# Nested self-attention on one core: a piece for 512- and 480-row pairs that runs on in class 448, and order lists with written-out PSUM banks

## The chip, the cores and the metric

The kernel runs on one core of one Trainium2 chip. The metric is the device time of one launch in microseconds; lower is better. The time of the kernel before is the median of three runs on the chip.

## What is computed

Thirty-two sequences of 64 to 511 valid rows, each 512 wide, go through a self-attention of 8 heads of 64 with one fused projection matrix. Rows behind a sequence's length are zero in the output.

```python
for b in range(batch):
    seq_len = lengths[b]
    x_b = x[b, :seq_len].copy()
    qkv = np.matmul(x_b, w_qkv)
    q, k, v = np.split(qkv, 3, axis=-1)
    ...
    scores = scale * np.matmul(q, k.transpose(0, 2, 1))
    scores_max = np.max(scores, axis=-1, keepdims=True)
    attn = np.exp(scores - scores_max)
    attn = attn / (np.sum(attn, axis=-1, keepdims=True) + 1e-08)
    out_b = np.matmul(attn, v).transpose(1, 0, 2).reshape(seq_len, dim)
    output[b, :seq_len] = out_b
```

The kernel takes the exponential without subtracting a maximum. The sums come out of the product with `v`, which carries a column of ones.

## The kernel before, in words

**Pairs and classes.** The device sorts the lengths in falling order and handles the sequences two at a time: pair p holds ranks 2p and 2p+1, and the first of the two is called batch 0 (or the first half), the second batch 1 (the second half). A pair's class is the longest length rounded up to one of 15 sizes (`CLASSES`: 512, 480, 448, ..., 96, and 340 between 352 and 320). For each class there is unrolled code for one pair. The lengths of this draw, sorted, are 502 447 | 446 436 | 363 357 | 351 347 | 343 333 | 323 315 | 310 261 | 260 257 | 246 230 | 223 220 | 216 183 | 164 152 | 143 140 | 134 119 | 101 86 | 79 75, so the pairs run in classes 512, 448, 384, 352, 352, 340, 320, 288, 256, 224, 224, 192, 160, 160, 128 and 96.

**A half.** `make_body(N, M, W)` writes the program of a pair for TensorE, ScalarE and VectorE. N is the row count at which batch 0 is worked, M that of batch 1, W that of the batch after it. In each half, the attention of the current batch is interleaved with the projections (Q, K and V) of the next one. There are three bodies for a class: `stay` (N, N, N), `leave` (N, N, next lower class) and, for some classes, `drops` (N, lower, lower), which works batch 1 already in the lower class. In the kernel before a drop exists where the lower class has as many 128-row tiles and N is at most 384; here pairs 4 (352 to 340), 5 (340 to 320), 6 (320 to 288), 10 (224 to 192) and 11 (192 to 160) take one. The function `graph` lays the pieces out and branches between them by a code per pair that is read from a table (2 × class, plus 1 for a drop). On TensorE, a jump can be announced ahead by a branch hint.

**Order of the work.** Inside a half the order is a hand-written string of tokens (`ORDER`, `DENSE`, `FOUR`), the same for all three engines; each engine runs its own instructions of it strictly in that order. `S` is the score matmuls of a unit and the exp on ScalarE that reads them; `D` the same for the dense three-tile classes, where both score slots are filled at once; `Q`, `K` project one of Q and K for one of the four pairs of heads, `B` both of them in one bank (two-tile classes); `E` and `F` to `I` are a projection of Q and K that is split in two by rows of the contraction (64 rows each, two matmuls side by side in the array); `V` projects one tile of V; `A` (and `Z`) are the products with V; `R` and `X`, the reciprocal and the multiplication on VectorE; `O` issues the store of half a batch from ScalarE's queue and reads the index of the batch it goes to (L1522 to L1527); reading the next pair's code is L1241 to L1245.

**PSUM and waits.** `psc` holds two score slots, s0 and s1; four more banks, a0, a1, v0 and v1, take projections and products with V. Whoever empties a bank raises its semaphore `e_<bank>`, and the next group of matmuls that writes the bank waits for it (`acquire`). In three- and four-tile classes up to 448 rows, the banks are handed out by turns: `pick` takes the first (with `~` the second) of a list, `give` puts the bank at its end, and the list runs on from the first half into the second. A group that starts a half thus gets the bank that was used longest ago. Classes 512 and 480, and the two-tile classes, use a0 and a1 for projections and v0 with v1 for products with V. In a two-tile half the scores of the next batch's first pair of heads are worked ahead: the units are pairs 1, 2, 3 and then 0 of the next batch.

**Moving data.** SyncE issues the loads of x, the transposing DMAs and the zero fills; GpSimd casts x and writes the ones. The change leaves both as they are, but for one constant in GpSimd's set-up.

The lines that the steps below touch: L324 is every matmul (`mm`), L367 and L408 the exps, L439 and L440 the copies of Q and K out of PSUM on ScalarE and VectorE, L463, L559 and L560 the masked copies of V, L638, L659 and L661 reciprocal and multiplication, L1527 the store.

## Time and profile before

| what | value |
|---|---|
| time, median of 3 runs | 333.07 us (332.78 to 334.8) |
| span of the profiled execution | 330.1 us; its own time is not among the three, and 333.07 less 330.1 leaves 3.0 us around the span |
| TensorE busy | 316.4 us, 96% of the span |
| ScalarE busy | 242.4 us, 73% |
| VectorE busy | 203.6 us, 62% |
| granted TensorE clock, mean | 0.991 |
| first pair (512) | 24.56 to 62.84 us |
| pair 1 (448) | 62.84 to about 98 us |
| seven dense halves (340 to 288) | 159.7 to 235.4 us |
| six two-tile pairs (256 to 160) | 235.4 to 310.7 us |

In a timeline row stand the start, the duration, the engine (a small q marks its sequencer), the line, the operation, out<-in, and the shapes; an x4 merges four instructions. The end of a matmul is modelled and overlaps the next, so the time that a group takes on TensorE is read from its start to the start of the next group. Rows of windows give busy time and count of each engine, then the granted clock, the DMA share and the traffic.

### The profile page before, as it was taken

To read this page: it belongs to the slowest core of one execution; us is meant where nothing else is said; L and a number is where in the kernel's file an instruction comes from. 1 tells how busy PE (TensorE), PEld (TensorE's weight loads), DVE (VectorE), ACT (ScalarE), POOL (GpSimd) and SP (SyncE) were. 2 spreads that over 40 slices of the span, in tenths; PEclk is the share of its full clock that TensorE was granted. 3 is DMA by queue.
4 is the path that set the end of the run, shared out by engine and by line. 5 is a ranking of instruction groups with operands and counts; after the bars stand their busy time and mean duration, and the time that the engine had idled before them with its cause. 6 is when DMAs were issued, how large, how long until landed. Compare 5 with 4: busy or idle time off the path is not lost. (4 is left out here: it accounts for less than half of the span.)

```text
span 330.1 us, 12320 instructions
## 1 busy us (share of the span) xinstructions
PE 316.4 (96%) x4353; PEld 205.5 (62%) x4354; DVE 203.6 (62%) x587; ACT 242.4 (73%) x358; POOL 68.7 (21%) x135
## 2 busy tenths in 40 slices
PE   7899999999999999999999999999999999999880
PEld 2565445455565656656666677677777777677750
DVE  3576576656585575576476557655755566767662
ACT  4577878788889879878778887787677676566531
POOL 3452220201111201210220222022111131131331
PEclk9999999999999999999999999999999999999996
DMA  6957599987656996985997999897689979965952
GB/s 195 341 138 263 94 375 310 292 179 279 153 194 142 326 263 145 323 286 149 283 314 169 235 319 216 214 291 235 212 139 174 214 199 183 170 201 148 200 145 70
DMA packets 83289, 72.42 MB, mean 219 GB/s; under 512 B 41660, under 2 KB 64188, under 8 KB 83204
## 3 DMA queue, kind: packets, MB, share of 16 engines
q1 hardware_dynamic: 69700, 58.27, 70.0%
q10 hardware_dynamic: 13504, 13.11, 11.8%
q8 instruction: 42, 0.69, 0.8%
q14 instruction: 43, 0.35, 0.4%
HBM read 25.32 MB, written 36.70 MB: 188 GB/s over the span
## 5 line engine op out<-in xcount | busy, mean ns | idle before, releaser
L367 ACT ACTIVATE ep<-psc 128x896 f16<-128x896 f32 (+9 forms) x184 | 146.8, 847 | 44.0 <-PE psc L324 34.0
L324 PE MATMUL pa<-xT,w_r 128*128 128x160 f16 (+19 forms) x952 | 127.8, 277 | 1.2 <-PEq L62 1.2
L324 PEld LDWEIGHTS pa<-xT,w_r 128*128 128x128 f16 (+1 forms) x952 | 73.0, 97 | 29.2 <-issue 10.1
L324 PE MATMUL psc<-qkT 64*128 64x224 f16 (+17 forms) x700 | 66.7, 285 | 0.6 <-ACT ep L408 0.4
L324 PE MATMUL pa<-w_r,xT 128*128 128x512 f16 (+4 forms) x332 | 58.6, 328 | 0.3 <-DVE v_aug L560 0.3
L324 PE MATMUL pav<-xT,w_r 64*128 64x352 f16 (+12 forms) x384 | 58.3, 306 | 0.0
L440 DVE CAST qkT<-pa 128x512 f16<-128x512 f32 (+9 forms) x59 | 33.4, 566 | 40.0 <-PE pa L324 36.2
L408 ACT ACTIVATE ep<-psc 128x864 f16<-128x864 f32 (+3 forms) x56 | 49.7, 946 | 10.9 <-PE psc L324 6.5
L324 PE MATMUL pav<-v_aug,ep 128*128 128x65 f16 x1268 | 54.9, 194 | 1.7 <-PEq L62 1.7
L1968 POOL MEMSET v_aug<- 128x256 f16 x28 | 8.8, 313 | 225.5 <-POOLq L1519 225.5
L324 PEld LDWEIGHTS pav<-v_aug,ep 128*128 128x128 f16 x1268 | 48.8, 98 | 10.0 <-issue 3.0
L439 ACT CAST qkT<-pa 128x320 f16<-128x320 f32 (+8 forms) x74 | 34.2, 466 | 16.6 <-PE pa L324 10.8
L661 DVE SCALAR_TENSOR_TENSOR onat<-pav,masks,rcp 128x128 f32<-128x128 f32 (+1 forms) x120 | 41.4, 384 | 4.1 <-DVE rcp L638 1.6
L1962 POOL CAST x<-x_nat 128x1536 f16<-128x1536 f32 (+3 forms) x33 | 42.0, 1272 | 8.6 <-POOLq L1519 8.3
L324 PEld LDWEIGHTS psc<-qkT 64*128 64x128 f16 x700 | 26.7, 94 | 27.2 <-issue 16.7
L463 DVE TENSOR_TENSOR v_aug<-pa,masks 128x512 f16<-128x512 f32 (+1 forms) x46 | 30.8, 674 | 15.0 <-PE pa L324 14.4
L324 PEld LDWEIGHTS pav<-xT,w_r 64*128 64x128 f16 (+1 forms) x384 | 29.8, 95 | 11.6 <-issue 1.6
L324 PEld LDWEIGHTS pa<-w_r,xT 128*128 128x128 f16 (+2 forms) x332 | 22.9, 99 | 18.3 <-issue 4.9
L324 PE MATMUL pav<-w_r,xT 128*128 128x512 f16 (+3 forms) x132 | 24.0, 333 | 0.0
L638 DVE RECIPROCAL rcp<-pav 128x8 f32<-128x8 f32 (+2 forms) x66 | 12.9, 195 | 17.5 <-PE pav L324 14.7
L324 PEld LDWEIGHTS pa<-v_aug,ep 128*128 128x128 f16 x524 | 19.3, 98 | 6.3 <-issue 2.6
L440 DVE CAST qkT<-pav 128x352 f16<-128x352 f32 (+7 forms) x27 | 14.4, 539 | 14.1 <-PE pav L324 13.4
(99 smaller groups left out, 181.4 us busy)
## 6 DMA issues: line engine op xcount, KB each, us to landing
out_dram<-zt SPq DMA_DIRECT2D x16, 768.0 KB, 5.7
x_nat<-in_x_dram SPq DMA_DIRECT2D x12, 512.0 KB
out_dram<-onat ACTq DMA_DIRECT2D x21, 256.0 KB, 3.8
x_nat<-in_x_dram SPq DMA_DIRECT2D x5, 1024.0 KB
out_dram<-onat ACTq DMA_DIRECT2D x12, 384.0 KB, 4.8
out_dram<-onat SPq DMA_DIRECT2D x12, 384.0 KB, 4.4
x_nat<-in_x_dram SPq DMA_DIRECT2D x17, 256.0 KB, 6.5
x_nat<-in_x_dram SPq DMA_DIRECT2D x4, 768.0 KB
```

Of the source, the lines that this page charges most:

```text
L324: return lambda e: e.matmul(o, lhsT, rhs, start=start, stop=stop)
L367: return e.activation(out=dst[at], in_=src[at], func=AF.Exp, scale=scale)
L408: lambda e, par=par, b=b: e.activation(out=ep[:, i, par, 0:T, 0:N], in_=psc_f[:, par, 0 : T * N].rearrange("p (t n) -> p t n", n=N), func= ...
L439: return lambda e: e.copy(out=dst, in_=src)
L440: return lambda e: e.tensor_copy(out=dst, in_=src)
L463: return lambda e: e.tensor_tensor(out=v_aug[h][:, t, lo // HD : lo // HD + n, 0:HD], in0=area[b][:, 0:w].rearrange("p (a d) -> p a d", d=HD),
L638: pr.add("dve", lambda e: e.reciprocal(out=rv, in_=den).then_inc(s_r, 1))
L661: ins = e.scalar_tensor_tensor(scalar=now[0][:, 1, t : t + 1], op0=ALU.mult, op1=ALU.mult, **ops)
L1962: e.tensor_copy(out=x16[h][:, 0:T, :], in_=x_nat[h][:, 0:T, :]).then_inc(s_xc[h], 1)
L1968: e.memset(v_aug[h][:, T - 1, NPAIR:NH, 0:HD], 0.0)
```

## The change

Every half is now written out with its banks. `LISTS` replaces `ORDER`, `DENSE` and `FOUR` for classes above 256 rows; `TWO` holds two lists for two-tile classes. A token names its banks behind a colon, and its engine by a letter (d VectorE, a ScalarE). The same list serves the first and the second half; `pick`, `give`, `turn` and the table of banks that was carried on are gone. The list of the dense classes, for example, has the banks that the turns gave to the first half before.

```diff
+    LISTS = {
+        512: "S e1:v0,a0 S E1da S e2:v1,a1 S c E2da S e0:v0,a0 S e3:v1,a1 S E0da E3da S S A00:v0 R00 X00 A01:a0 R01 X01 V1d:v1 A10:a1 R10 X10 S S A11:v0 R11 X11 V3d:a0 A20:v1 R20 X20 S O S V0d:a1 A21:v0 R21 X21 S A30:a0 R30 X30 A31:v1 R31 X31 S S V2d:a1",
...
+        288: "K2d:a0 Q2a:a1 D e1:v0,v1 e3:a0,a1 E1aa E3ad D K0a:v0 c A00:v1 R00 X00 Q0d:a1 A10:a0 R10 X10 D V2d:v0 O V1d:v1 A20:a1 R20 X20 D A30:v0 R30 X30 V0d:a0",
     }
-        4: "S S Q0 +A0 S S K0 V0 S S Q1 +A1 S S K1 V1 S S Q2 +A2 S S K2 V2 S S Q3 +A3 S S V3 K3 O",
-        2: "S S B0 b1 A0 A1 b2 S S V1 b3 A2 O A3 R3 X3 V0",
-    DENSE = "K2 q2 D E1 E3 I1 H3 D k0 c A0 Q0~ A1 D V2 O V1 A2 D A3~ V0"
-    DENSE_OUT = DENSE.replace("D A3~ V0", "V0 D A3")
+    TWO = {
+        False: "S1 S0 e0:a0,a1 e1:v0,v1 E0d E1d S2 S3 A00:a0 A01:a1 R0 X00 X01 V0d:v0 V1d:v1 A20:a0 A21:a1 R2 X20 X21 B2a:v0 c B3d:v1 O",
+        True: "S1 S0 e0:a0,a1 e1:v0,v1 E0d E1d S2 S3 V1d:a0 A00:v0 A01:v1 R0 X00 X01 B2a:s0 A20:a0 A21:a1 R2 X20 X21 V0a:v0 c B3d:v1 O",
+    }
```

In a two-tile half all four pairs of heads now have their scores in the half itself (S1 S0 first, S2 S3 later), two of the projections are split by rows (`two_cross`) and emptied two banks at a time by VectorE, and two pairs of heads share a bank for the product with V (`two_attn`). The second list is for batches whose last tile has at most 64 rows; there V0 is masked and copied by ScalarE (`v_out` and `vsides` have a form for it).

```diff
+    def two_cross(pr, h, i, bs, W, engs=None):
+
+        last = engs is not None
+        mms = [m for pair in zip(*(
+            qk_mms(bs[f], h, [(i, f)], W, MAXS, ROWS[f ^ last], not last, last)
+            for f in range(2)
+        )) for m in pair]
+        done, n = s_crossed[i], len(mms) - 2
+        if last:
+            pr.take("pe", done, 2)
+        else:
+            for b in bs:
+                acquire(pr, b)
...
+        eng = engs[0]
+        for b in bs:
+            pr.take(eng, full[(b, eng)])
+            pr.busy[b] = bs[0]
+        pr.joined.update({bs[0]: bs[1], bs[1]: bs[0]})
+        src, dst = two_banks(bs)[:, :, 0:W], qkT[h][:, 2 * i : 2 * i + 2, 0:W]
+        pr.add(eng, lambda e: (e.copy if eng == "act" else e.tensor_copy)(
+            out=dst, in_=src).then_inc(free[bs[0]], 1))
```

The part that gives the change its name: classes 512 and 480 get a drop to 448. The prologue marks the jump to the first of these pieces ahead.

```diff
-    drops = {N: make_body(N, lower[N], lower[N], turn=turn(N)) for N in CLASSES
-             if lower[N] < N and -(-lower[N] // P) == -(-N // P) and N <= 3 * P}
-    drops_to = [lower[N] for N in drops]
+    drops_at = {N: M for N, M in lower.items()
+                if M < N <= 3 * P and (-(-M // P) == -(-N // P))}
+    drops_at.update({N: FOUR_ROWS for N in CLASSES if N > FOUR_ROWS})
+    drops = {N: make_body(N, M, M) for N, M in drops_at.items()}
+    drops_to = list(drops_at.values())
...
+            if tok == "V2":
+                pr.add("pe", hint_drop)
...
+    def hint_drop(e):
+        e.reg_alu(regs["far"], regs[e.engine][1], 1, ALU.not_equal)
+        regs["opened"] = e.mark_branch_hint_location(regs["far"])
...
-        marks = {}
+        marks = {("tail", -1, 1): [regs["opened"]]} if fetch else {}
```

In this draw pair 0 (502 and 447 rows) takes the new piece. Its first half is worked at N = 512 and projects 448 rows of batch 1, its second half is class 448 throughout; before, the two halves were 512 with 512 rows projected, and 512 with 480.

Two places show how the order moved. The first is TensorE at the end of the first half of a 288-row pair (pair 7): the last V projection of the half and, behind the branch, the first projection of the second half. Names with _0 and _1 are the two batches' buffers; e_a0 and e_v1 are raised when those banks are empty. Before:

```order
L324 MATMUL pa<-w_r,xT_1 128x512 [waits e_a0]
L324 MATMUL pa<-w_r,xT_1 128x512 x3
L1311 REGISTER_ALU
L1312 BRANCH_PREFETCH_HINT
L1331 COMPARE_AND_BRANCH
L1311 REGISTER_ALU
L1312 BRANCH_PREFETCH_HINT
L1311 UNCONDITIONAL_BRANCH
L324 MATMUL pav<-xT_0,w_r 128x288 [waits s_xt0,e_v1]
L324 MATMUL pav<-xT_0,w_r 128x288 x3
L324 MATMUL pa<-xT_0,w_r 128x288 [waits e_a1]
```

The same place with the change:

```order
L333 MATMUL pa<-w_r,xT_1 128x512 [waits e_a0]
L333 MATMUL pa<-w_r,xT_1 128x512 x3
L1474 REGISTER_ALU
L1475 BRANCH_PREFETCH_HINT
L1494 COMPARE_AND_BRANCH
L1474 REGISTER_ALU
L1475 BRANCH_PREFETCH_HINT
L1474 UNCONDITIONAL_BRANCH
L333 MATMUL pa<-xT_0,w_r 128x288 [waits s_xt0,e_a0]
L333 MATMUL pa<-xT_0,w_r 128x288 x3
L333 MATMUL pa<-xT_0,w_r 128x288 [waits e_a1]
```

The V projection writes a0 in both; the K projection behind it took v1 and now takes a0 again. The matmuls are the same.

The second place is ScalarE in a first half of a pair in class 224, from the middle of the half to the first exps of the second half; idx and codes are the tables of batch indices and of class codes, s_of00 says that the first half of batch 0's output is complete. Before:

```order
L1241 ISA
L1245 TENSOR_LOAD codes
L367 ACTIVATE ep<-psc 128x2x2x224 [waits f_s0_act]
L367 ACTIVATE ep<-psc 128x2x2x224 [waits f_s1_act]
L439 CAST qkT_1<-pa 128x2x224 [waits f_a0_act]
L1522 ISA
L1523 TENSOR_LOAD idx
L1524 ISA
L1527 ISA [waits s_of00]
L1527 DMA out_0_dram<-onat_0 128x2x256
L1495 COMPARE_AND_BRANCH
L367 ACTIVATE ep<-psc 128x2x2x224 [waits f_s0_act]
```

With the change:

```order
L376 ACTIVATE ep<-psc 128x2x2x224 [waits f_s1_act]
L448 CAST qkT_1<-pa 128x2x224 [waits f_v0_act]
L1403 ISA
L1407 TENSOR_LOAD codes
L1694 ISA
L1695 TENSOR_LOAD idx
L1696 ISA
L1699 ISA [waits s_of00]
L1699 DMA out_0_dram<-onat_0 128x2x256
L1667 COMPARE_AND_BRANCH
L376 ACTIVATE ep<-psc 128x2x2x224 [waits f_s0_act]
L376 ACTIVATE ep<-psc 128x2x2x224 [waits f_s1_act]
```

The copy of a projection that stands ahead of the store is now that of B2, whose matmuls are the last but one group of the half; the code is read behind it and no longer two exps earlier. The exps behind the branch are those of S1 and S0, on which S2 and S3 of the same half wait on TensorE.

More of the change, by code (lines that the diff above doesn't have):

```diff
@@ L795, in half @@
-            return
-        per = T if T >= 3 else 1
-        ahead = tiles if T >= 3 else 1
-        units = [(i, k) for i in (1, 2, 3) for k in range(per)] + [(0, k) for k in range(ahead)]
-        norm, dones, both = {}, 0, []
-        dense, turns = is_dense(N), in_turns(N)
-        four = FOUR_SIDES if tiles == T and half_rows(W) else FOUR
-        toks = ((DENSE_OUT if tiles < T else DENSE) if dense else four if T == 4 and turns else ORDER[T]).split()
-        def pick(second=False):
-            if turns:
-                b = st["banks"].pop(1 if second else 0)
-                st["seen"].add(b)
-                st["holds"].pop(b, None)
-                return b
-            st["bank"] ^= 1
-            return f"a{st['bank'] ^ 1}"
@@ L938, in is_dense, with make_body @@
         return -(-N // P) == 3 and 3 * N <= 2 * MAXS
-    def in_turns(N):
-        return 2 * P < N <= FOUR_ROWS
-    def make_body(N, M, W, last=False, turn=None):
+    def make_body(N, M, W, last=False):
         T = -(-N // P)
         pr = Prog(CANON, 0)
-        first = ("v0", "a0", "v1", "a1") if T == 4 else tuple(area)
-        st = {"slot": 0, "bank": 0, "banks": list(first), "seen": set(), "holds": {}}
+        st = {"slot": 0, "seen": set(), "holds": {}, "two": False}
         for h in range(2):
@@ L1306, in graph @@
         drop = [N in drops for N in CLASSES]
+        to = [CLASSES.index(drops_at.get(N, lower[N])) for N in CLASSES]
         assert tiles[n - 3 :] == [2, 1, 1]
```

686 lines of the change are left out of this document (410 added, 276 removed), and 8 rows, old and new, of tables (LISTS, ORDER).

## The prediction

> **What bounds the kernel now.** I read the page's busy times first, then the windows by stage, then the timelines of TensorE, VectorE and ScalarE where the order changes.
>
> ```profile
> PE 316.4 (96%) x4353; PEld 205.5 (62%) x4354; DVE 203.6 (62%) x587; ACT 242.4 (73%) x358; POOL 68.7 (21%) x135
> ```
>
> ```profile
> 24.56:43.95 19.39, 19.39 (x210) 9.47 (x210) 12.42 (x28) 15.50 (x16) 4.31 (x4) 1.00 0.71 197
> 43.95:62.84 18.89, 18.89 (x209) 9.61 (x208) 12.48 (x34) 15.24 (x16) 2.29 (x3) 1.00 1.14 314
> 62.84:80.43 17.59, 17.57 (x245) 10.05 (x245) 10.89 (x33) 14.33 (x20) 2.29 (x3) 1.00 0.88 263
> ...
> 159.71:235.38 75.67, 75.06 (x1158) 53.30 (x1158) 47.44 (x157) 60.03 (x91) 12.51 (x19) 1.00 0.92 240
> 235.38:310.67 75.29, 74.96 (x1084) 56.62 (x1084) 47.93 (x128) 51.92 (x85) 17.86 (x36) 1.00 0.87 186
> ```
>
> The first number is the stretch, the second TensorE's busy time. In every stage the two are equal to within 0.6 us, at granted clock 1.00: TensorE never waits, and the other engines have a quarter or more of each stage to spare. Two things follow. What shortens TensorE's own work is gained in full. And every wait that the new order puts in front of a TensorE group is lost in full, since no slack is there to take it up. So I look at each piece for fewer columns, and for new waits.
>
> **The new 512 piece** (pair 0). It does less work. The first half of pair 1 (third row of the windows) is the same list at N = 448 with 448 rows projected: 17.59 us. The new second half is just that, 17.59 against 18.89: 1.30 gained. The new first half is that plus 64 more score columns in 24 matmuls. Pairs of them run side by side:
>
> ```profile
> 58.15 0.58 PE L324 MATMUL psc<-qkT 64*128 64x480 f16 x4
> 58.66 0.38 PE L324 MATMUL pa<-xT,w_r 128*128 128x480 f16 x1
> ```
>
> Four of 480 columns take 0.51 us, so 64 more columns in 24 take 24/4 x 0.51 x 64/480 = 0.41; 18.0 us against 19.39, 1.39 gained. Against that, the K copies (E1da, E2da, E0da, E3da) go to ScalarE, which before had exps alone there:
>
> ```profile
> 67.43 0.54 ACT L439 CAST qkT<-pa 128x448 f16<-128x448 f32 x1
> ```
>
> The 15.50 us of 16 exps in the first row of the windows (0.97 each) and four such copies are 17.7 us in 18.0: nearly full. The first seven exps and two copies are 7 x 0.97 + 1.08 = 7.9 us, while TensorE brings seven score units in about 7 us; two slots of buffer leave a wait of some tenths, which I put at 0.3 (0 if the queue keeps up, 1.0 if it starts late). The piece gives 1.30 + 1.39 - 0.3 = **-2.4 us**. Pair 1 has the same list and the same turn of banks as before: 0.
>
> **The dense halves** (340 to 288 rows, seven in all). The matmuls are the same. But one list now serves both halves, and it ends with V0 in bank a0 and begins with K2 in bank a0. K2 has to wait until VectorE has copied V0 out, behind the last product's reciprocal and multiplications. Before, the turns gave K2 another bank. The old trace tells when that copy ends, since VectorE's order is unchanged. Here are TensorE's K2 behind the end of the first second half and of a first half, the same for the last of each, and then VectorE's copies of V0 (L463) at these four places:
>
> ```profile
> 170.25 1.25 PE L324 MATMUL pa<-xT,w_r 128*128 128x320 f16 x8
> ...
> 181.66 0.71 PE L324 MATMUL pav<-xT,w_r 128*128 128x320 f16 x4
> ```
>
> ```profile
> 214.47 1.14 PE L324 MATMUL pa<-xT,w_r 128*128 128x288 f16 x8
> ...
> 225.16 0.60 PE L324 MATMUL pav<-xT,w_r 128*128 128x256 f16 x4
> ```
>
> ```profile
> 170.83 0.69 DVE L463 TENSOR_TENSOR v_aug<-pav,masks 128x512 f16<-128x512 f32 x1
> ...
> 181.97 0.69 DVE L463 TENSOR_TENSOR v_aug<-pa,masks 128x512 f16<-128x512 f32 x1
> ```
>
> ```profile
> 215.25 0.69 DVE L463 TENSOR_TENSOR v_aug<-pav,masks 128x512 f16<-128x512 f32 x1
> 225.49 0.69 DVE L463 TENSOR_TENSOR v_aug<-pa,masks 128x512 f16<-128x512 f32 x1
> ```
>
> The copy ends at 171.52, K2 began at 170.25: 1.27 us. Likewise 1.47, 1.00 and 1.02. Second halves mean 1.37, first halves 1.01, and there are three boundaries of each kind between the seven halves: 3 x 1.37 + 3 x 1.01 = **+7.1 us**. Behind K2 on TensorE stand q2 and the next D, so the whole engine waits; ScalarE's exps follow D. The lower bound is 0 if the copy were early, which nothing here suggests; the upper, with a release and a refill of the array per wait, some 8. Into the first dense half, Q2 takes a1 behind V2 in a1:
>
> ```profile
> 159.04 0.74 PE L324 MATMUL pa<-xT,w_r 128*128 128x340 f16 x4
> ```
>
> ```profile
> 158.77 0.69 DVE L463 TENSOR_TENSOR v_aug<-pa,masks 128x512 f16<-128x512 f32 x1 [0.45 <-PE pa L324]
> ```
>
> 159.46 - 159.04 = **+0.4**. In the other three-tile classes one more projection and two score units lie between the two uses: 0 (0.1 a half at worst).
>
> **The two-tile halves** (twelve, pairs 8 to 13). Columns are equal again. The split projections spare changes between 64-row and 128-row use of the array, some 0.1 us each; what decides is a loop that the new order closes. S2 and S3 need the slots of S1 and S0, so they wait for exps that start the half. Those stand on ScalarE behind the copy of B2, the code load and the store. How long that takes, from the end of one half to the start of the next (class 224):
>
> ```profile
> 248.77 0.53 ACT L439 CAST qkT<-pa 128x448 f16<-128x448 f32 x1
> ...
> 249.03 1.49 ACTq L1527 DMA_DIRECT2D out_dram<-onat  x2
> ...
> 250.91 1.73 ACT L367 ACTIVATE ep<-psc 128x896 f16<-128x896 f32 x2 [1.61 <-PE psc L324]
> ```
>
> From copy to exp 2.14 us: two stores with the index load between, then the branches. At the end of a first half there is one store, but both loads:
>
> ```profile
> 255.69 0.54 ACT L439 CAST qkT<-pa 128x448 f16<-128x448 f32 x1
> 256.62 0.39 ACTq L1527 DMA_DIRECT2D out_dram<-onat  x1
> ```
>
> ```profile
> L1245 ACTq TENSOR_LOAD <-codes x6: 284/292/457, 239.4 to 303.2; - x6
> ```
>
> 257.01 - 255.69 = 1.32, plus 0.3 for the code and 0.2 for the branch: 1.8. Before, this delay was free: the pair needed first had its exps a half earlier. TensorE's pieces at 224 rows, start to start:
>
> ```profile
> 249.93 0.56 PE L324 MATMUL psc<-qkT 64*128 64x224 f16 x8
> 250.42 1.71 PE L324 MATMUL pa<-xT,w_r 128*128 128x224 f16 x16
> 251.97 0.65 PE L324 MATMUL pav<-v_aug,ep 128*128 128x65 f16 x16
> 252.46 0.93 PE L324 MATMUL pa<-xT,w_r 128*128 128x224 f16 x8
> ...
> 253.81 1.04 PE L324 MATMUL pa<-w_r,xT 128*128 128x512 f16 x4
> 254.69 0.93 PE L324 MATMUL pa<-xT,w_r 128*128 128x224 f16 x8
> 255.45 0.65 PE L324 MATMUL pav<-v_aug,ep 128*128 128x65 f16 x16
> ...
> 256.90 0.56 PE L324 MATMUL psc<-qkT 64*128 64x224 f16 x8
> ```
>
> The loop, from one first exp to the next: two exps 1.73, S3 0.25, A00 and A01 0.49, V0 and V1 2 x 0.88, A20 and A21 0.49, B2 0.76, two handovers 0.2, then 1.8 or 2.14: 7.5 or 7.8 us. A half took 256.90 - 249.93 = 6.97. So +0.67 on the mean, where TensorE alone would need about 6.75. Classes 192 and 160 use the second list, with V0 on ScalarE last:
>
> ```profile
> 288.52 0.45 PE L324 MATMUL psc<-qkT 64*128 64x160 f16 x8
> ...
> 291.66 0.63 PE L324 MATMUL pa<-w_r,xT 128*64 128x256 f16 x8
> 292.22 0.73 PE L324 MATMUL pa<-xT,w_r 128*128 128x160 f16 x8
> 292.79 0.65 PE L324 MATMUL pav<-v_aug,ep 128*128 128x65 f16 x16
> ...
> 300.13 0.45 PE L324 MATMUL psc<-qkT 64*128 64x160 f16 x8
> ```
>
> ```profile
> 300.87 1.30 ACT L367 ACTIVATE ep<-psc 128x640 f16<-128x640 f32 x2 [1.66 <-PE psc L324]
> ```
>
> 1.30 + 0.19 (S3) + 0.56 (V1) + 0.49 + 0.57 (B2) + 0.49 + 0.88 (V0) + 0.2 + 1.8 or 2.14 is 6.5 or 6.8, against (300.13 - 288.52)/2 = 5.80: +0.85. Four boundaries have the first list, seven the second: 4 x 0.67 + 7 x 0.85 = **+8.6 us**. Both ends: -2 in all if the exps start on time (TensorE's own pace), +13 if each load and branch is as slow as the longest. I take the loop, since its terms are all rows of the same stage. Entering the stage, e0 takes a0 behind the V0 of the last dense half: 1.0 to 1.5 us of copy, 0.5 of S1 and S0 ahead of it, **+0.7**. Leaving it, the last scores wait for B3's copy: +0.4, most of it in a wait that is there anyway, none if all.
>
> **The sum.** -2.4 + 7.1 + 0.4 + 8.6 + 0.7 + 0.4 = +14.8 us. On the span that is 330.1 to 344.9; with the 3.0 us around it, as in the median run, 333.07 to **347.9 us**, 4.4% slower. One per cent, 3.3 us, is about what a measurement of this kernel can tell from no change.
>
> **Rivals.** (1) The bank waits come, but the exps start on time, because ScalarE's queue is read ahead while a copy runs (that it is, the first store 0.26 us after the copy's start shows). Then two-tile halves run at TensorE's pace, 12 x -0.2: -2.4 + 7.5 + 0.7 - 2.4 = +3.4, 336.5 us. Against it: the 2.14 us already contain this reading ahead. (2) Faster: the split projections leave TensorE no change of array use where it had two, and the new piece is shorter, while VectorE empties V0 in time. -2.4 - 2.4 = -4.8, 328.3 us. It decides only if K2's wait is under some 0.2 us a boundary; the rows say 1.0 to 1.5. (3) The change doesn't do what it says: pair 0's second batch, 447 rows, doesn't get the new code, and the 512 list with 512 rows projected runs: no gain from the piece, 350.3 us. Against it: 447 is below 448, and the table is built from that comparison. (4) The clock: TensorE, with waits in each half, loses its full clock. The last stage speaks against it:
>
> ```profile
> 317.46:323.00 5.54, 3.62 (x67) 2.60 (x67) 3.75 (x7) 2.22 (x5) 1.33 (x3) 1.00 0.45 120
> ```
>
> With TensorE busy 65% and waits of up to 1 us, it kept 1.00. If the clock did fall to half over a tenth of the two-tile stage's 75 us, 7.5 us more: 355 us. The Trainium skill, "TensorE: Matmul & The Clock Gate" (section "HAM oscillation — how this bites in real kernels"), lets the clock fall only for idle stretches beyond about 3.4 us, but its next section tells of frequent short idling on PSUM that brought it down too. By the first rule the time is my sum, by the second this rival; the row agrees with the first.
>
> **How the numbers follow.** Forecast 0.68, with its own range of 342 to 353; rival 1 0.16, rival 2 0.05, rival 3 0.04, rival 4 0.07. The range 336 to 353 holds the forecast, half of rival 1's neighbourhood and rival 3. Slower by over 1% (above 336.4): 0.68 + 0.04 + 0.07 and most of rival 1, 0.90. Within 1%: the rest of rival 1 and a little of 2, 0.06. Faster by over 1%: 0.04.
>
> **What would show it.** TensorE idle 1.0 to 1.5 us ahead of K2's first matmul at six dense boundaries, released by VectorE's masked copy of V0; S2 or S3 waiting for an exp in each two-tile half, halves of 7.5 and 6.6 us; pair 0 in about 36 us for 38.28. I am wrong if K2 follows V0 without a gap, if the first exp of a two-tile half starts within 0.5 us of its scores, or if pair 0 takes as long as before.

## The result, and the profile after

The changed kernel takes **367.38 us** (median of 4 runs, 367.04 to 367.55), beside 333.21 us before (332.78 to 334.8): a ratio of 1.103, interval 1.0996 to 1.1055. Slower was forecast, but by 14.8 us; it is 34.2. 367.38 lies outside the range of 336 to 353.

The page of the kernel after, its busy times and the row of the granted clock (40 slices of 9.1 us, in tenths):

```profile
PE 324.6 (89%) x4617; PEld 209.3 (57%) x4618; DVE 208.1 (57%) x625; ACT 238.8 (65%) x348; POOL 68.4 (19%) x137
...
PEclk9998999899999999999999999999999999989997
```

TensorE fell from 96% busy to 89%, though its busy time rose by 8 us. The clock dips inside the program at two places of the first quarter and at one near 320 us, in the two-tile pairs; before, only the end had such a dip. Where the time went is read from windows whose borders are the same event in both programs: TensorE's first score of pair 0, of pair 1, of pair 2, of the dense classes, of the two-tile classes, and of the classes behind them. (Stretch, length, then busy time and count of TensorE, its weight loads, VectorE, ScalarE and GpSimd, the clock, the DMA share and GB/s.) Before:

```profile
24.56:62.84 38.28, 38.28 (x416) 19.09 (x416) 24.90 (x61) 30.75 (x32) 6.60 (x7) 1.00 0.92 255
62.84:98.15 35.31, 35.29 (x494) 20.45 (x494) 22.72 (x70) 29.66 (x39) 4.62 (x7) 1.00 0.75 223
98.15:157.19 59.04, 59.00 (x849) 36.01 (x849) 36.18 (x109) 49.37 (x79) 9.41 (x15) 1.00 0.80 231
157.19:235.38 78.19, 77.58 (x1176) 54.50 (x1174) 49.48 (x163) 61.40 (x93) 13.08 (x21) 1.00 0.93 245
235.38:310.67 75.29, 74.96 (x1084) 56.62 (x1084) 47.93 (x128) 51.92 (x85) 17.86 (x36) 1.00 0.87 186
310.67:330.06 19.39, 9.78 (x173) 7.04 (x172) 8.96 (x19) 5.13 (x11) 5.42 (x12) 0.85 0.44 126
```

After, with two more windows (first and third) in which TensorE does nothing at all:

```profile
24.26:29.62 5.36, 0.00 (x1) 0.01 (x2) 1.23 (x4) 0.00 (x0) 1.43 (x1) 0.99 1.04 355
29.62:66.63 37.01, 37.01 (x488) 20.84 (x488) 21.17 (x66) 31.19 (x39) 5.23 (x7) 0.95 0.87 248
66.63:69.01 2.38, 0.00 (x1) 0.01 (x2) 0.69 (x1) 0.69 (x1) 0.00 (x0) 1.00 0.62 216
69.01:105.76 36.75, 36.75 (x492) 21.15 (x493) 21.86 (x68) 29.95 (x38) 4.62 (x7) 0.95 0.56 165
105.76:166.25 60.49, 59.73 (x849) 36.05 (x849) 36.15 (x109) 49.51 (x79) 9.26 (x15) 1.00 0.79 229
166.25:252.26 86.01, 78.73 (x1175) 53.69 (x1173) 49.94 (x164) 61.41 (x93) 13.02 (x21) 1.00 0.77 227
252.26:346.90 94.64, 81.12 (x1277) 58.70 (x1277) 55.91 (x161) 46.47 (x67) 17.46 (x36) 0.98 0.53 144
346.90:365.86 18.96, 9.77 (x172) 7.05 (x172) 7.75 (x16) 5.14 (x11) 5.36 (x12) 0.86 0.38 116
```

A clock of 0.95 in a stretch of 37 us is 3.41 us at half speed, with TensorE busy throughout: 1.7 us lost. Taken apart, against the terms of the prediction:

| part | measured, us | forecast |
|---|---|---|
| TensorE empty at the jump into the new piece (0 to 5.36; it began 0.3 earlier) | +5.1 | 0 |
| pair 0 itself, 38.28 to 37.01, without the clock | -3.0 | -2.4 |
| TensorE empty at the jump out of it | +2.4 | 0 |
| pair 1, 35.31 to 36.75, without the clock | -0.3 | 0 |
| pairs 2, 3 and half of 4 | +1.4 | 0 |
| dense halves, 78.19 to 86.01 | +7.8 | +7.5 |
| two-tile halves, 75.29 to 94.64, without the clock | +17.7 | +9.7 |
| three dips of the clock | +5.1 | 0 |
| the rest | -0.4 | 0 |
| sum (span 330.1 to 365.9) | +35.8 | +14.8 |

**The jumps.** TensorE's timeline around them, before and after. In the bracket stands the idle time ahead of the row; "issue" says that the trace shows nothing that it waited for:

```profile
23.50 1.06 PE L324 MATMUL pa<-w_r,xT 128*128 128x128 f16 x16
24.56 0.61 PE L324 MATMUL psc<-qkT 64*128 64x512 f16 x4
...
61.94 0.97 PE L324 MATMUL pa<-xT,w_r 128*128 128x480 f16 x4
62.84 0.36 PE L324 MATMUL psc<-qkT 64*128 64x448 f16 x2
```

```profile
23.82 0.44 PE L333 MATMUL pa<-w_r,xT 128*128 128x128 f16 x5
29.62 0.61 PE L333 MATMUL psc<-qkT 64*128 64x512 f16 x2 [5.36 <-issue]
...
65.59 1.04 PE L333 MATMUL pa<-w_r,xT 128*128 128x512 f16 x4
69.01 0.36 PE L333 MATMUL psc<-qkT 64*128 64x448 f16 x2 [2.38 <-issue]
```

On TensorE's sequencer the branch (L1510) stands from 23.88 for 5.68 us and from 65.54 for 3.41; the same two branches took 0.42 and 0.35 before. A transfer of an instruction queue, 16 KB, starts behind each jump, at 27.0 and 66.6. That fits an engine that fetches code which isn't there yet, though the trace doesn't say for which engine a transfer is. The Trainium skill, "Runtime: NRT & Kernel Launch" (section "Instruction fetch mechanics"), says that a taken branch out of the pages at hand has to fetch its target before it goes on; the trace fits that, and adds the price.

**The dense halves** do what was forecast. TensorE at the end of the first of them, then VectorE there, then all waits of the dense stage by releaser (total, times, longest):

```profile
178.94 1.02 PE L333 MATMUL pa<-w_r,xT 128*128 128x512 f16 x4
181.13 1.12 PE L333 MATMUL pa<-xT,w_r 128*128 128x320 f16 x7 [1.17 <-DVE v_aug L482]
```

```profile
180.39 0.69 DVE L482 TENSOR_TENSOR v_aug<-pa,masks 128x512 f16<-128x512 f32 x1
```

```profile
PE pa L333 <- DVE v_aug L482: 6.8, 7, 1.4
```

V0's copy ends at 181.08, and K2 follows 0.05 later. The six gaps are 1.17, 0.89, 1.25, 0.89, 1.35 and 0.89; the seventh, 0.32, is Q2 at the entry.

**The two-tile halves.** TensorE in one half of class 224, ScalarE at its start:

```profile
268.32 0.56 PE L333 MATMUL psc<-qkT 64*128 64x224 f16 x8
268.71 1.89 PE L333 MATMUL pa<-xT,w_r 64*128 64x224 f16 x32
270.83 0.37 PE L333 MATMUL psc<-qkT 64*128 64x224 f16 x4 [0.23 <-ACT ep L376]
271.64 0.37 PE L333 MATMUL psc<-qkT 64*128 64x224 f16 x4 [0.44 <-ACT ep L376]
...
276.28 0.56 PE L333 MATMUL psc<-qkT 64*128 64x224 f16 x8
```

```profile
267.71 0.53 ACT L448 CAST qkT<-pa 128x448 f16<-128x448 f32 x1 [2.37 <-ACTq L63]
267.97 1.50 ACTq L1699 DMA_DIRECT2D out_dram<-onat  x2
269.86 3.34 ACT L376 ACTIVATE ep<-psc 128x896 f16<-128x896 f32 x4 [1.62 <-ACTq L63]
```

From the copy to the first exp 2.15 us (2.14 forecast); S2 and S3 wait, and the half takes 7.96 (7.5 to 7.8 forecast). With the second list, in class 160, the same chain is much longer:

```profile
314.45 0.45 PE L333 MATMUL psc<-qkT 64*128 64x160 f16 x8
314.74 1.57 PE L333 MATMUL pa<-xT,w_r 64*128 64x160 f16 x32
318.04 0.31 PE L333 MATMUL psc<-qkT 64*128 64x160 f16 x4 [1.73 <-ACT ep L376]
...
324.10 0.45 PE L333 MATMUL psc<-qkT 64*128 64x160 f16 x8
```

```profile
314.19 0.69 ACT L475 ACTIVATE v_aug<-pa,masks 128x512 f16<-128x512 f32 x1 [1.62 <-ACTq L63]
314.43 2.50 ACTq L1699 DMA_DIRECT2D out_dram<-onat  x2
317.29 2.49 ACT L376 ACTIVATE ep<-psc 128x640 f16<-128x640 f32 x4 [2.41 <-issue]
```

From the copy to the first exp 3.10 us, since the two stores, with the index load between them, took 2.50 of issuing here, and the half 9.65 (it also has the third dip of the clock). The other halves in class 160 took 7.16 to 7.77, where 6.5 to 6.8 was forecast and 5.80 was the old time.

### The profile page after: what moved, and what is told of

The parts are those of the page before. It is cut to its first block, busy times and chain, and to the rows that moved or that the text cites. A ratio compares the mean times of both kernels' runs of the same rounds, so it can differ in the third digit from the quotient of the medians.

```text
span 365.9 us, 12983 instructions
## 1 busy us (share of the span) xinstructions
PE 324.6 (89%) x4617; PEld 209.3 (57%) x4618; DVE 208.1 (57%) x625; ACT 238.8 (65%) x348; POOL 68.4 (19%) x137
## 3 DMA queue, kind: packets, MB, share of 16 engines
q10 hardware_dynamic: 13504, 13.11, 10.9%
## 5 line engine op out<-in xcount | busy, mean ns | idle before, releaser
L376 ACT ACTIVATE ep<-psc 128x896 f16<-128x896 f32 (+8 forms) x184 | 144.8, 843 | 52.9 <-PE psc L333 29.8
L333 PE MATMUL pa<-xT,w_r 64*128 64x448 f16 (+21 forms) x1536 | 140.2, 286 | 9.8 <-DVE v_aug L482 7.7
L333 PEld LDWEIGHTS pa<-xT,w_r 64*128 64x128 f16 (+1 forms) x1536 | 83.7, 96 | 51.8 <-DVE v_aug L482 12.8
L333 PE MATMUL psc<-qkT 64*128 64x448 f16 (+16 forms) x700 | 70.7, 287 | 19.2 <-ACT ep L376 9.7
L449 DVE CAST qkT<-pa 128x448 f16<-128x448 f32 (+8 forms) x79 | 42.2, 543 | 72.4 <-PE pa L333 69.7
L333 PEld LDWEIGHTS pa<-v_aug,ep 128*128 128x128 f16 x1792 | 63.7, 98 | 19.2 <-issue 9.8
L333 PE MATMUL pa<-v_aug,ep 128*128 128x65 f16 x1792 | 71.2, 195 | 2.1 <-PEq L63 1.9
L448 ACT CAST qkT<-pa 128x288 f16<-128x288 f32 (+8 forms) x76 | 33.1, 470 | 30.2 <-ACTq L63 15.9
L617 DVE SCALAR_TENSOR_TENSOR onat<-pa,masks,rcp 128x128 f32<-128x128 f32 x136 | 41.5, 344 | 4.0 <-DVE rcp L600 1.3
L600 DVE RECIPROCAL rcp<-pa 128x6 f32<-128x6 f32 (+1 forms) x80 | 14.8, 185 | 14.8 <-PE pa L333 13.5
L781 DVE SCALAR_TENSOR_TENSOR onat<-pa,masks,rcp 128x256 f32<-128x256 f32 x36 | 16.2, 478 | 1.8 <-DVE rcp L767 0.8
L475 ACT ACTIVATE v_aug<-pa,masks 128x512 f16<-128x512 f32 x7 | 4.8, 689 | 10.9 <-PE pa L333 5.8
```

What stands on the lines that cost most here:

```text
L333: return lambda e: e.matmul(o, lhsT, rhs, start=start, stop=stop)
L376: return e.activation(out=dst[at], in_=src[at], func=AF.Exp, scale=scale)
L448: return lambda e: e.copy(out=dst, in_=src)
L449: return lambda e: e.tensor_copy(out=dst, in_=src)
L600: pr.add("dve", lambda e: e.reciprocal(out=rv, in_=den).then_inc(s_r, 1))
L617: ins = e.scalar_tensor_tensor(scalar=now[0][:, 1, t : t + 1], op0=ALU.mult, op1=ALU.mult, **ops)
```

## The experiments

All are timed beside the kernel before on the same chip (332.4 to 333.1 us).

**The drop of 512 taken out.** Theory: the piece costs more by its jumps than it spares. Rival: the start stalls with or without the piece.

```diff
-    drops_at.update({N: FOUR_ROWS for N in CLASSES if N > FOUR_ROWS})
...
-            if tok == "V2":
-                pr.add("pe", hint_drop)
```

> The changed kernel without its drop of classes 512 and 480 (pair 0 runs in its own class with the new 512 list, as a stay-then-leave body; the mark ahead is gone with it); everything else as changed. The changed kernel's trace shows two jumps of TensorE's queue that took 5.68 and 3.41 us (before: 0.42 and 0.35), and the granted clock at 0.5 for some 3.3 us behind each (1.7 us of work lost). Theory: the jump into the far piece costs what the trace shows. Then this kernel gains 5.3 + 3.1 + 2 x 1.7 = 11.8 us and loses what the piece gave, 2.5 us: about 358 us for 367.4, both jumps under 0.7 us. Rival: the start would have stalled anyway, because x's loads keep the DMA engines full from 24 to 28 us; then the first wait of 5 us stays in front of the first or second group of pair 0, and the time is 363 or above.

367.2 us (363.14 to 368.25), ratio 1.104, interval 1.098 to 1.110: nothing gained. The jump into pair 0 now costs no gap, but the next one does:

```profile
61.29 1.04 PE L333 MATMUL pa<-w_r,xT 128*128 128x512 f16 x4
67.89 0.56 PE L333 MATMUL psc<-qkT 64*128 64x448 f16 x2 [5.56 <-issue]
```

The branch out of pair 0 takes 6.65 us, though it is marked ahead, and another dip follows at 67.2. No jump into the piece is left here, yet a jump stalls: what I called the price of the piece can fall on another jump, and this edit only changed which one it was.

**K2 in another bank.** Theory: the dense loss is K2 behind V0's copy. Rival: K2 waits there for something else, which comes no earlier.

```diff
-        288: "K2d:a0 Q2a:a1 D e1:v0,v1 ...
+        288: "K2d:v1 Q2a:a1 D e1:v0,v1 ...
```

The same in 320 and 340.

> The changed kernel with one bank changed in the three dense lists: K2 at the head goes to v1 in place of a0, so that it does not follow V0 into the same bank. Theory (the prediction's term): the six waits of 0.9 to 1.4 us ahead of K2 are the bank's; they go, and the time falls by 6 to 7 us, to about 361. Rival: K2 waits there for something else that comes no earlier (the transposed x, or the branch); then the gaps stay and the time is 367. A second one: v1 is late too, since V1's copy is behind the masked work of VectorE; then 2 to 4 us are gained.

360.7 us (357.3 to 363.2), 1.076 (1.069 to 1.083): 6.7 less than after by the medians. The dense stage, same borders:

```profile
166.18:245.54 79.36, 78.07 (x1177) 55.22 (x1174) 49.42 (x164) 61.63 (x93) 13.05 (x21) 1.00 0.86 236
```

79.36 for 86.01, and all six gaps are gone, which refutes the rival; 1.2 us are left over the old 78.19.

**Store and code ahead of the last groups.** Theory: the two-tile loss is ScalarE's chain of copy, code, stores and first exps. Rival: the bank waits and the split projections of the lists.

```diff
-        False: "... V0d:v0 V1d:v1 A20:a0 A21:a1 R2 X20 X21 B2a:v0 c B3d:v1 O",
-        True: "... B2a:s0 A20:a0 A21:a1 R2 X20 X21 V0a:v0 c B3d:v1 O",
+        False: "... V0d:v0 V1d:v1 c O A20:a0 A21:a1 R2 X20 X21 B2a:v0 B3d:v1",
+        True: "... B2a:s0 c O A20:a0 A21:a1 R2 X20 X21 V0a:v0 B3d:v1",
```

In the second list V0 is masked here with the row of the batch that follows in place of its own, since `O` raises ScalarE's rank, so the output is not right; the instructions are the same.

> The changed kernel with the tokens c and O (reading the code, index and store on ScalarE) moved ahead in the two-tile lists: in the first list behind V1, ahead of B2's copy; in the second behind B2's copy, ahead of V0's. Nothing else moves. Theory: the two-tile halves are a closed loop through ScalarE's queue (copy, code, index, store, branch, first exp); with the 1.3 to 2.5 us of loads and stores out of the loop, S2 and S3 wait no more for late exps, a half of class 160 takes 6.4 to 6.8 us for 7.2 to 8.1 (and 9.65 once), and the time falls by 8 to 14 us, to 354 to 360; the dip of the clock at 320 us goes with the wait ahead of it. Rival: the halves are long because of bank waits (A20 behind V1's copy out of a0, V0 behind the multiplication out of v0) and of the split projections; then under 3 us are gained.

357.4 us (354.05 to 357.91), 1.071 (1.063 to 1.078): 10 less than after. The two-tile stage:

```profile
255.07:336.56 81.49, 77.03 (x1278) 58.17 (x1277) 56.18 (x161) 47.24 (x67) 17.63 (x36) 1.00 0.71 173
```

81.49 for 94.64. Of the 13.15, 1.7 is a dip that didn't come; 11.4 was the chain. No score waits for an exp any longer, yet the stage is 6.2 above the old 75.29: the rival holds for that part.

**Projections whole again.** e3, with ScalarE's mask row put right, and B0 and B1 each in one bank in place of the split pair. Theory: the split, which the prediction had sparing time, costs some.

```diff
-        False: "S1 S0 e0:a0,a1 e1:v0,v1 E0d E1d S2 S3 ...
+        False: "S1 S0 B0d:v0 B1d:v1 S2 S3 ...
```

> The kernel of e3 (c and O ahead; V0's mask now the right row) with the two split projections of a two-tile half made whole again: B0 in v0 and B1 in v1, 16 matmuls of 128 rows for 32 of 64. Measured for the split in e3 at 160 rows: 1.34 us from the first of them to S2, for 1.14 of the 16 whole ones before the change. Theory: the split costs time in place of sparing it; 0.2 us a half are gained, 2 to 3 us in all, to 355 for 357.4. Rival (the prediction): whole projections cost two changes of the array's use more; then it is 1 to 2 us slower, 359. S2 may start before the second exp is done: a wait of up to 0.4 us a half would show it.

352.74 us (351.86 to 356.77), 1.064 (1.056 to 1.071). The stage:

```profile
252.84:332.51 79.67, 76.81 (x1085) 57.20 (x1085) 57.19 (x161) 47.06 (x67) 18.57 (x36) 1.00 0.77 175
```

1.8 us less than e3. Of this, 0.6 is not the split: in e3 the first split projection of the stage waits 0.63 us in a0 for V0's copy out of the last dense half, and B0 in v0 doesn't. So the split costs at most 1.2 us, 0.1 a half. (The median fell by 4.7, but the two jumps differ as well: 4.94 and 4.15 us in e3, 3.17 and 6.20 here.)

**V1 in bank a1.** e3 with the mask row put right, and V1 moved so that A20 need not wait for its copy. Rival: the wait goes to the next user of the bank.

```diff
-        True: "... S2 S3 V1d:a0 A00:v0 ...
+        True: "... S2 S3 V1d:a1 A00:v0 ...
```

> The kernel of e3 (V0's mask the right row) with V1 in a1 in place of a0 in the second two-tile list, so that A20, which takes a0, has not to wait until VectorE has copied V1 out. Theory: A20 stood up to 0.4 us behind B2 for that copy; A21 comes 0.25 us later, so some 0.2 to 0.3 us a half of eight halves go: 1.5 to 2.5 us, to 355.5. Rival: the next in the chain, V0 behind the multiplication out of v0, takes the wait over, and the time stays at 357.

355.66 us (355.31 to 355.84), 1.068 (1.065 to 1.072). The gap ahead of A20 is gone; three gaps of 0.31 to 0.47 stand ahead of V0 instead (0.22 and 0.23 in e3), and the stage takes 81.67 (e3: 81.49). The rival holds.

**Earlier marks.** The first mark is put where the codes are read, two marks 6.2 us ahead of the second jump.

```diff
-            if tok == "V2":
-                pr.add("pe", hint_drop)
             if tok == "Q2":
                 pr.add("pe", lambda e: begin_loops(e))
+                pr.add("pe", hint_drop)
...
+                at = body.wide(body.second[name], len(body.ops["pe"]))[-3] + 1
+                body.run_part(e, body.second[name], at, None,
+                              lambda: expect("drop", k, codes))
```

> The changed kernel with its two marks for the new piece moved: the mark for the jump into it stands behind the reading of the codes (15.4 us in the trace of the change) in place of 1.8 us ahead of the jump, and the marks for the jump out of it stand in the middle of its second half, 9 us ahead, in place of the end of its first half, 17.5 us ahead. Theory: both jumps stall because the code isn't there, the first because its mark comes too late for a fetch of 5 to 7 us, the second because what was fetched is gone again after 500 further instructions. Then both jumps fall under 0.7 us, the clock stays, and the time falls by 9 to 12 us, to 355 to 358. Rival: fetches wait behind x's loads whatever the mark; then the first jump stays above 3 us (and only the second falls), 362 to 364. A third: marks do nothing for these jumps, 367.

366.9 us (364.04 to 367.87), 1.101 (1.093 to 1.108): a miss. The first jump now takes 0.37, the second still 3.51. And some 5 us later TensorE waits 1.26 us for a copy of VectorE, which jumped too, and stood empty from 25.59 to 29.20. Later 2.3 us are lost in the two-tile stage (two dips there, for one). The mark works; it isn't the only thing late.

**All repairs.** The mark at the codes, two marks for the second jump at the first wide matmul of the second half, K2 in v1, the early store with the right mask row.

> The changed kernel with all repairs: K2 in v1 (dense lists), c and O ahead in the two-tile lists (and ScalarE's masked copy of V0 reads the row of the batch that it had before), the mark for the jump into the new piece behind the reading of the codes, and the marks for the jump out of it behind the first split projection of the second half. Theory: -6.7 (dense), -10 (two-tile), -5.3 and a clock dip of 1.7 (first jump) from 367.4: 343.7; if the mark a page ahead brings the code of class 448 in time, the second jump falls from 3.4 to 0.4 us and takes its dip of the clock with it: 339. Rival for the second jump: a mark is lost when the queue goes on into another page of code, whatever the place; then it stays at 3.4 us or above (6.7 as without a drop).

346.08 us (344.54 to 348.87), 1.040 (1.033 to 1.047). The repairs add up: 21 us of the 34. The second jump still takes 3.99, with a dip of 6.83 us behind it.

**The title's part alone.** The kernel before with the drop from 512 to 448, for which classes 512 and 480 get the list of class 448, and with these marks; the other lists and their turns are untouched.

```diff
-        return 2 * P < N <= FOUR_ROWS
+        return 2 * P < N
...
+    for N in CLASSES:
+        if N > FOUR_ROWS:
+            drops_at[N] = FOUR_ROWS
+            drops[N] = make_body(N, FOUR_ROWS, FOUR_ROWS)
```

> The kernel before with only what the title says: classes 512 and 480 get the list of 448 (FOUR, by turns) and a drop to 448; the mark for the jump into the piece behind the reading of the codes, those for the jump out of it behind the first split projection of the second half; no other list is touched. Theory: the piece alone gains 2 to 3 us in pair 0 (36 us for 38.3), and with both jumps under 0.7 us the time is 330 to 331.5. If the second jump stalls 3.4 us (and the clock dips behind it, 1.7), 333 to 336. Rival: the split lists are no faster at 512 rows, and pair 0 takes as long as before: 333.

339.7 us (338.24 to 340.77), 1.020 (1.015 to 1.024): 6.7 us *slower* than the kernel before, for a piece that does less work. TensorE at the two places that matter:

```profile
31.22 0.53 PE L324 MATMUL pav<-xT,w_r 64*128 64x448 f16 x1 [2.65 <-DVE qkT L440]
...
67.49 0.36 PE L324 MATMUL psc<-qkT 64*128 64x448 f16 x2 [2.30 <-issue]
```

VectorE is late after its own jump (2.65), the second branch takes 3.38, and the clock dips at 31.09 and 68.64. No list behind pair 0 was changed, so all of this belongs to the drop with its list.

**One mark, or two, at one place.** From f1, the marks of the second jump go behind the third split projection of the second half. f2 marks one target (the code of the next pair in class 448), f3 two.

```diff
-                body.run_part(e, body.second[name], None, lambda: expect("drop", k, codes))
+                at = body.wide(body.second[name], len(body.ops["pe"]))[2] + 1
+                body.run_part(e, body.second[name], at)
+                expect("drop", k, codes[2:])
+                body.run_part(e, at, None)
```

> The kernel before with the drop (f1), but for the jump out of the new piece only one mark in place of two (that of the code that is taken, 4), and it stands behind the third split projection of the second half, some 15 us ahead. In all kernels so far the second jump stalled 3.4 to 6.7 us, whether its marks stood 17.5, 16 or 6 us ahead, and TensorE's instruction fetch of 16 KB began behind the jump; the kernel before had one mark 15.8 us ahead and a jump of 0.35 us. Theory: two marks in a row spoil each other, or a mark has to stand in the page of 256 instructions ahead of the one that holds the jump; with one mark there the second jump falls to 0.4 us, the dip of the clock goes, and the time is 334 to 335.5 for 339.7. Rival: class 448's code is too far away, and marks don't serve there; then 339 to 340.

> The same kernel with both marks at the place where f2 has one. If two marks spoil each other, the jump stalls 3.4 us or more here, and does not in f2; if the place decides, it falls to 0.4 us in both, and the times are equal; if marks don't serve there, it stalls in both.

f2: 335.94 us (334.39 to 338.65), 1.011 (1.005 to 1.018). f3: 338.87 us (334.25 to 339.58), 1.010 (1.001 to 1.020). The times don't tell them apart, and each trace is of one run. In the traces, with one mark the second branch takes 0.37 and no dip is there, with two it takes 3.34 and the clock dips at 31.07 and 68.62. What spoils it may be the second mark or the compare-and-branch that stands between the two; nor is it a rule, since in the kernel before two such marks (202.50 and 202.83) stood ahead of a jump that took 0.46. f2 is still not faster than before: TensorE waits 2.14 us for VectorE behind the first jump, and 1.44 for ScalarE, which has a jump of its own, behind the second. ScalarE there:

```profile
65.75 3.35 ACT L367 ACTIVATE ep<-psc 128x896 f16<-128x896 f32 x4 [2.26 <-issue]
```

**The piece laid elsewhere.** f5 and e8 were meant to put the piece's code next to class 448. The blocks of the built programs come out in the old order, so f5 is f1 again, block for block, and e8 is e5 with whole projections and V1 in a1.

> The kernel before with the drop (f1) and its code laid out in the order in which this draw runs it: the piece of 512 to 448 right behind the start, then the classes from 448 down, and those of 512 and 480 at the end (a draw whose first pair doesn't drop would pay for that). Theory: the new piece itself is worth 2 to 3 us, and all that it lost came from code that TensorE, VectorE and ScalarE had to fetch at two jumps: VectorE's first copy comes at 27 us in place of 30, no wait of 2.65 us behind it, the second jump takes 0.4 us, no dip of the clock before 320 us; 330 to 331 us for 339.7 (and 333.0 of the kernel before). Rival: the waits are not the code's, and the time stays over 336. A second: the stalls go, but the piece gives nothing, 333.

> The changed kernel with all repairs together: K2 in v1; c and O ahead in the two-tile lists; whole projections B0 and B1; V1 in a1 in the second list; the mark behind the codes; code laid out as in f5. Theory (the sum of what each gave): e5's 346.1, -3 (whole projections), -1.7 (V1), -4 (second jump) -1.3 (VectorE's start) -3 (dips of the clock): 333 to 335, the kernel before give or take one per cent: nothing of the 34 us is left without a place. Rival: some 3 us or more remain that no repair touched (the three-tile classes with their split projections, banks in the first two-tile list): 337 to 340.

f5: 338.38 us (336.34 to 340.17), 1.015 (1.008 to 1.022); its second branch took 6.56 us, where that of f1 took 3.38. e8: 344.44 us (342.49 to 345.67), 1.034 (1.027 to 1.040), with 6.33. Whether nearness of the code would help stays untried; what the pair shows is how far one stall varies.

**Both jumps mended, alone and with the rest.** g1 is the changed kernel with the mark at the codes and the one mark of f2. g2 adds K2 in v1, the early store, whole projections and V1 in a1.

> The changed kernel with nothing mended but the two jumps of TensorE: the mark for the first behind the reading of the codes, and one mark (for code 4) behind the third split projection of the second half in place of two at the end of the first half. Theory: both jumps take 0.4 us (5.68 and 3.41 before), the two dips of the clock behind them go (2 x 1.7 us), and two waits of 1 to 2 us come in, since VectorE and ScalarE fetch their own code at both jumps without a mark: 367.4 - 5.3 - 3.1 - 3.4 + 2.7 = 358, 356 to 361. Rival: one mark serves only in the old kernel's layout of pages, and the second jump stalls 3 us or more here too: 363.

> The changed kernel with everything mended that has a name: the jumps as in g1, K2 in v1, c and O ahead in the two-tile lists, whole projections B0 and B1, V1 in a1. Theory: e8 (344.4) less its jump of 6.3 us and its dip of 3.4, plus a wait of 1.4 us for ScalarE's code: 336 to 337.5; left over the old kernel: some 2.5 us of VectorE's and ScalarE's code at the jumps, 1.7 us of bank waits in the classes of 384 and 352 rows, 2 us of the two-tile lists, less 2.5 us that the piece gives. Rival: the second jump stalls as in e8, 342 or more; or something of 3 us and more is left that has no name, and no jump stalls.

g1: 363.1 us (359.81 to 367.24), 1.088 (1.080 to 1.095); its profile is that of the longest of its runs. g2: 343.18 us (341.66 to 346.25), 1.030 (1.026 to 1.033). Both miss what was expected, by 5 and 6 us. TensorE's branches are short now (0.79 and 0.37 in g1, 0.37 and 0.35 in g2), and the wait behind the second has only changed its name. TensorE, ScalarE and VectorE in g2:

```profile
67.56 0.56 PE L333 MATMUL psc<-qkT 64*128 64x448 f16 x2 [3.56 <-ACT ep L376]
```

```profile
66.58 2.54 ACT L376 ACTIVATE ep<-psc 128x896 f16<-128x896 f32 x3 [4.03 <-issue]
```

```profile
67.14 1.16 DVE L449 CAST qkT<-pa 128x448 f16<-128x448 f32 x2 [4.34 <-issue]
```

ScalarE and VectorE stand empty for over 4 us, waiting for nothing that the trace shows, both just behind the same jump (in g1 4.17 and 5.56). That they fetch their code there is the likely cause, and not shown. Before, ScalarE had a wait of 1.08 there, for TensorE's scores. The clock then drops for two periods (66.29 to 73.12 at 0.50). No version was faster than the kernel before.

## Why the prediction was wrong

**The step that failed** is one that the working doesn't have. "The prologue marks the jump to the first of these pieces ahead", says the change, and that mark was costed at nothing; that the piece is reached and left by jumps into other code was not costed at all. The part on the new piece went straight from windows of matmuls to -2.4 us. Measured, the jumps cost TensorE 5.1 + 2.4 us, and two of the three dips, 3.4 us, follow them: 10.9 us. The old branches, under 0.7 us but for one of 1.20 near the end (323.25), gave no price for a jump that stalls. An operation that the trace doesn't show had to be bounded from both sides, and wasn't. That the drop with its list causes such a loss by itself, f1 shows (+6.7); that mending one jump exposes another, or another engine's, e1, e4, g1 and g2 show. A second step failed in size, TensorE's pace in the two-tile halves (below).

**The new piece: right.** 35.3 us without the dip for 38.28, 3.0 less where 2.4 was forecast. ScalarE kept up, so the 0.3 for its queue wasn't needed, though the working read its slack too wide: in four of its five rows ScalarE is busy 79 to 81%, which leaves a fifth and not a quarter. Rival 3 is refuted with it: the second batch was worked at 448.

**The dense halves: right, mechanism and size.** 7.8 for 7.5. Gaps of 1.17, 1.25 and 1.35 at second halves (1.37 forecast) and 0.89 three times at first halves (1.01), released by V0's copy; e2 removed them all, and its stage is 6.65 shorter.

**The three-tile classes: mis-sized.** "0 (0.1 a half at worst)" measured +1.4 us over five halves. Two split projections wait 0.35 and 0.32 us for banks that the turns would have handed out later; the other 0.7 is busy time that I could not place.

**The two-tile halves: the wait right, TensorE's pace under it of the wrong sign.** The 8.6 us were the loop less the old halves, and the working put TensorE's own pace, with no waits at all, 0.2 us a half *below* the old one, because the split spares changes of array use. So 8.6 + 2.4 = 11.0 us of waiting on ScalarE were in it, and e3 took 11.4 away; with the first list the chain fits too (2.15 us for 2.14). What failed is the pace: e3 shows 81.49 us where no exp is waited for, 6.2 above the old stage. Of this, 1.2 at most is the split itself (e6), 0.6 the entry (0.7 forecast), about 1.0 the last scores' wait for B3's copy (1.05 in e6; 0.4 forecast), and the rest, some 3 us, small bank waits and matmuls less well packed, I could not separate. With the second list the sum left out that A20 waits in a0 for V1's copy and V0 in v0 for the multiplications, and took the short stores; by the first scores of each half, and without the dip, its seven halves lost some 1.9 us each (0.85 forecast). Rival 1 is refuted, since the exps start late, and since without that wait the stage is still longer than before; rival 2 as well.

**The clock (rival 4): came in part.** I let one row decide, in which TensorE kept its full clock at 65% busy, and gave the rival 0.07. That row was right but told less than I took from it. The clock fell after idle times of 2.38 and 1.73 us, with nothing near 3.4 us, against the rule that I cited from the Trainium skill, "TensorE: Matmul & The Clock Gate" (section "HAM oscillation — how this bites in real kernels"). What the traces show of it is told below.

**The whole.** Of the 21.0 us between 14.8 and 35.8, the jumps make 7.5, the dips 5.1, the two-tile halves 8.0, the three-tile classes 1.4, the dense ones 0.3; the better piece gives 0.6 back, pair 1 and the rest 0.7. Why a mark serves in f2 and not in f3, nor in e1, where one mark stood alone as in the kernel before, and why such a stall takes anything from 3.2 to 6.7 us (3.38 in f1, 6.56 in f5, the same program), stays open. So does what ScalarE and VectorE would do with their code at hand, which wasn't tried.

## What to carry to other kernels

A new piece of code is not only its instructions: on each engine that has to jump to it, ask whether its code is at hand, and look for a branch on the sequencer that lasts microseconds, or an idle time with "issue" and no releaser. When a list replaces banks that were handed out by turns, take each bank's next user and the last emptying in front of it, row by row; this priced the dense halves to within 0.3 us. Where the bound engine has no slack, removing a wait shows the next one, so expect repairs to give less than the gap that they close.

## What the runs showed of the chip

**A jump into code that is not at hand** cost 3.2 to 6.7 us on TensorE, and left ScalarE empty for 2.3 to 4.2 and VectorE for 3.6 to 5.6, where the old jumps on TensorE took under 0.7, but for one of 1.20. That the code was missing is inferred from the transfers of the instruction queues. With one mark some 15 us ahead TensorE's second jump took 0.35 to 0.37 (f2, g1, g2), with two it took 3.34 (f3), and one mark 17.8 us ahead didn't help (6.65 in e1).

**The clock goes by periods of a grid, not by the length of an idle time alone.** All dips of a program begin on one grid of 3.41 us (29.55, 70.51 and 319.68 in the kernel after lie 12 and 73 periods apart), and TensorE was busy for little of the period ahead of each. These are pairs of periods of the kernel after, the one ahead and the one behind:

```profile
22.72:26.14 3.42, 1.54 (x28) 1.36 (x25) 2.24 (x6) 0.26 (x1) 0.00 (x0) 1.00 0.71 215
26.14:29.55 3.41, 0.00 (x0) 0.00 (x0) 0.00 (x0) 0.00 (x0) 1.36 (x1) 1.00 1.06 352
67.10:70.51 3.41, 1.50 (x16) 0.70 (x18) 0.47 (x1) 1.20 (x3) 0.66 (x3) 1.00 0.51 166
70.51:73.92 3.41, 3.41 (x22) 1.32 (x20) 1.16 (x2) 1.77 (x2) 1.64 (x1) 0.50 0.43 79
316.27:319.68 3.41, 1.39 (x26) 0.83 (x25) 0.80 (x3) 2.40 (x4) 0.10 (x1) 1.00 0.59 130
319.68:323.09 3.41, 3.41 (x41) 2.86 (x38) 2.54 (x9) 0.52 (x2) 0.00 (x0) 0.50 0.56 173
```

Busy for 1.50 and 1.39 us (44 and 41%), the clock fell; busy for 1.54 (45%), it did not. In the traces of all runs every period at full clock with TensorE busy for less than 45% was followed by a dip, none above 57% was, and in between both happened: 1.94 us (57%, at 299.20) was not followed by one, 1.93 in e1 (at 299.30) was, and of 1.83 and 1.86 in e4 the first was and the second was not. So the share doesn't decide alone, and what else does stays open. Nor does the length of the idle time: in e7 TensorE stood empty for 3.65 us, up to 27.69, over two periods of the grid that were each busy 46 to 47%, and the clock stayed. A gap of 1.7 us, badly placed on the grid, can be enough, and it costs 1.7 more. The Trainium skill's "TensorE: Matmul & The Clock Gate" (section "Part 1: The HAM clock gate (the "warmup" mystery)") has a free-running window of about 3.4 us; the grid agrees with it, and the zone of 45 to 57% is what these runs add.

**A store on ScalarE's queue** took from 0.38 us to 1.40 us of issuing (at 315.52; the row of 2.50 at 314.43 is two stores and the index load between them), which in a chain without slack goes straight into TensorE's wait.
